# A planned encoder trunk: ScalarE table sets placed by hand, transfers that may be issued from SyncE or from GpSimd, and one large buffer less

## The chip, the cores and the metric

The kernel runs on one core of a Trainium2 chip. The metric is the device time of one execution in microseconds; the kernel before takes 1237.68 us (median of 3 runs, 1236.67 to 1237.9). A core has TensorE (PE; its weight loads are shown as PEld), VectorE (DVE), ScalarE (ACT), GpSimd (POOL) and SyncE (SP). Each has an instruction stream of its own, worked off in order; they meet through semaphores.

## The reference

A two-layer bidirectional encoder trunk on x of 1 x 512 x 1024 in float32. In each layer four token mixers of 256 channels each read the same normed input: a diagonal complex state-space layer in both directions (S5), a convolution module with a gate, latent attention (MLA) and grouped-query attention (GQA). Their outputs are normed, joined and projected into the residual stream. Then follows a gated MLP with a width-3 convolution.

```python
def reference(x, ...):
    for i in range(DEPTH):                                   # 2
        h = rms_norm(x, attn_norm_g[i])
        u_s5, conv_in, q_lat, kv_lat, k_pe, q_g, k_g, v_g = jnp.split(h @ w_in[i], IN_SPLIT_POINTS, axis=-1)
        y_s5 = s5_mixer(u_s5, ...)                           # scan, gelu, y * sigmoid(y @ w_glu + b)
        y_conv = conformer_conv(conv_in, ...)                # val * sigmoid(gate), conv k=31, layer norm, silu
        y_mla = mla_mixer(q_lat, kv_lat, k_pe, ...)          # 4 heads, softmax
        y_gqa = gqa_mixer(q_g, k_g, v_g, ...)                # 4 heads on 2 key heads, softmax
        mixed = rms_norm(jnp.stack([y_s5, y_conv, y_mla, y_gqa], axis=2), mix_norm_g[i])
        x = x + mixed.reshape(bsz, seq_len, MIX_WIDTH) @ w_out[i]
        h = rms_norm(x, ffn_norm_g[i])
        x = x + conv_ffn(h, ...)                             # (silu(gate) * up) @ w_down, 2816 wide
    return rms_norm(x, final_norm_g)
```

## The kernel before

Activations are held transposed, features on the 128 partitions and the 512 tokens along the free dimension, so x is eight tiles of 128 x 512. Every large product is made from three matmuls in fp32r: each operand is split into a rounded high part (`copy`) and the rest (`tensor_sub`), and high x high, high x low and low x high are added up in PSUM (`mm3`, line 688). In the MLP, from the fourth of 22 pairs of tiles on, a product of 2 x 2 blocks is done with seven block products (`quarters`, line 1441).

Nothing is issued where it is written. Each call on `V`, `A`, `T`, `X` or `G` (VectorE, ScalarE, TensorE, SyncE's DMA queue, GpSimd) adds an operation with an estimated cost to a plan (`_cost`, line 550). `copy` (line 750) adds one operation with two alternatives, ScalarE or VectorE. `run` (line 210) makes up to 10 schedules, forwards and backwards in turn, and keeps the one whose estimated span is shortest. `forward` (line 309) goes through the engines in the order A, V, T, X, G whenever one is free, takes the operation with the highest priority that is ready, and gives buffers to its outputs: 51 small ones (515 words a partition), 22 large ones (1024 words), 16 tiny ones and 8 PSUM banks. A small tile may take a large buffer when the small ones are out. `emit` (line 516) then issues everything in that order. All instructions therefore carry the line of `emit` (L529) in the profile; they are told apart by their tiles: `v_s`, `v_b` and `v_t` are small, large and tiny buffers, `bank` is PSUM, `xs__65` is x, `vec__67` and `c_sb` are constants.

ScalarE's functions come in table sets. `SETS` (line 129) tells the planner which functions share one; a function of another set costs 1300 ns in the plan, and its operation is held back as if its priority were 4000 ns lower (`SWITCH`). The loads themselves are not in the plan's order: the library puts one ahead of an activation whose function is not in the set that is loaded. An rstd (`rstd_of`, line 736) is a Ln followed by an Exp.

A layer has two stages. `mixing` projects and runs the four mixers, interleaved by the planner, then four group norms and the output projection. `ffn` norms x, makes the operands of the block products from r (`operands`, line 1415) and goes through the 22 pairs; in layer 0 it also carries the preparation of the next layer's S5 weights. In layer 1 the last down projection, the final norm and the output are in `finish` (line 1513), in two halves of 256 tokens.

The transfers in the mixing stages that matter below are these: the window loads of the S5 weights from DRAM (`s5_front`, `s5_out`), the copies that put the parts of each head's q and k into one tile (`gqa`, `mla`), and the shifted windows of the convolution's input (`conv`). All DMAs are issued from SyncE. GpSimd does memsets only.

## Time and profile before

| | |
|---|---|
| median of 3 runs | 1237.68 us |
| the profiled execution | 1237.17 us, its span 1235.3 us |
| mean granted TensorE clock | 0.991 |
| instructions | 19839 |
| DMA | 144.64 MB, mean 117 GB/s |
| share of the chain that ended last | PE 75%, DVE 17%, ACT 3%, issue 2%, DMA 2% |

The stages in the span: mixing of layer 0 up to about 240 us with its output projection to 262, the MLP of layer 0 to about 600, mixing of layer 1 to about 865, the MLP of layer 1 to 1222 with the final norm behind it. The planner lets them overlap at their edges.

Busy time of TensorE is the union of matmuls whose ends are modelled, so it does not show small gaps; the waits of its weight loads do. A row of waits has: engine, tile and line, who was waited for, us in total, how often, longest. A row by groups has: line, engine, operation, out<-in with shapes, how many, busy us and mean ns of one, idle us before them and what ended it. A window row has: start and end, its length, then busy us and instructions of PE, PEld, DVE, ACT and POOL, the granted clock, the busy share of the DMA engines and GB/s.

### The profile page before, as it was taken

The numbers are of one execution on the slowest core, as the hardware profiler recorded it, in microseconds if no ns is written. First come the engines' busy times: TensorE is split into PE (matmuls) and PEld (weight loads), VectorE is DVE, ScalarE is ACT, GpSimd is POOL, SyncE is SP. The second block draws the span as 40 slices with busy tenths as digits, with TensorE's granted clock in tenths as the row PEclk, the third lists the DMA queues.
The fourth block names the chain that finished last, engine by engine and source line by source line (L and its number), as shares of the span: only waits on it lengthen the run. The fifth ranks groups of instructions, "written<-read, shape, count | busy, mean of one in ns | idle before, by whom it ended". The sixth has DMA issues, their size and how long they took to land.

```text
span 1235.3 us, 19839 instructions
## 1 busy us (share of the span) xinstructions
PE 1194.5 (97%) x7144; PEld 976.1 (79%) x7144; DVE 1126.1 (91%) x2220; ACT 751.4 (61%) x1383; POOL 6.9 (1%) x27
## 2 busy tenths in 40 slices
PE   7999999999999999989999999999999799999996
PEld 5874466788999998978878746658899699999986
DVE  8999989869999999999987998886999998989876
ACT  6458699746657565646473277984666455656444
POOL 0000000000000000000000000000000000000000
PEclk9999999999999999989999999999999899999998
DMA  8568491402333323214466147522033233333202
GB/s 319 137 208 264 96 247 39 137 18 86 103 93 97 110 95 111 83 56 138 163 218 199 26 122 183 148 95 68 26 111 120 95 103 95 111 92 120 80 1 68
DMA packets 88962, 144.64 MB, mean 117 GB/s; under 512 B 22176, under 2 KB 34976, under 8 KB 88736
## 3 DMA queue, kind: packets, MB, share of 16 engines
q1 hardware_dynamic: 88864, 143.38, 37.8%
q8 instruction: 56, 0.92, 0.3%
q14 instruction: 42, 0.34, 0.1%
HBM read 118.96 MB, written 13.89 MB: 108 GB/s over the span
## 4 chain that ended last, share of the span: by engine, by line
PE 75%; DVE 17%; ACT 3%; issue 2%; DMA 2%; SPq 0%; DVEq 0%; ACTq 0%
PE bank L529 75%; DVE v_s L529 13%; DVE v_b L529 3%; ACT v_s L529 2%; ACT L529 1%; DVE xs__65 L529 1%; DMA y_d<-v_b 0%; DMA v_s<-y_d 0%; ACT v_b L529 0%; DMA xs__65<-in_xT_dram 0%; DMA v_b<-in_w_out_dram 0%; DMA v_b<-in_w_dn_dram 0%; DMA v_s<-in_w_dn_dram 0%; SPq L529 0%; DVE v_t L529 0%
## 5 line engine op out<-in xcount | busy, mean ns | idle before, releaser
L529 PE MATMUL bank<-v_b,v_s 128*128 128x256 f32 (+3 forms) x3390 | 582.0, 294 | 9.6 <-DVE xs__65 L529 8.7
L529 PEld LDWEIGHTS bank<-v_b,v_s 128*128 128x128 f32 (+1 forms) x3390 | 480.3, 189 | 37.4 <-DVE xs__65 L529 10.3
L529 DVE TENSOR_TENSOR v_s<-v_s,v_s 128x512 fp32r<-128x512 f32 (+6 forms) x709 | 440.8, 654 | 10.6 <-ACT v_s L529 6.7
L529 PE MATMUL bank<-v_s,v_s 128*128 128x512 f32 (+2 forms) x1455 | 433.1, 379 | 7.2 <-ACT v_s L529 2.6
L529 PE MATMUL bank<-v_s,v_b 128*128 128x512 f32 (+3 forms) x1480 | 358.2, 414 | 10.1 <-ACT v_b L529 8.9
L529 PEld LDWEIGHTS bank<-v_s,v_s 128*128 128x128 f32 (+1 forms) x1455 | 250.0, 185 | 62.5 <-issue 5.3
L529 PEld LDWEIGHTS bank<-v_s,v_b 128*128 128x128 f32 (+2 forms) x1480 | 221.5, 172 | 96.0 <-issue 36.3
L529 ACT CAST v_s<-v_s 128x512 fp32r<-128x512 f32 (+1 forms) x386 | 223.5, 604 | 104.4 <-DVE v_s L529 77.4
L529 ACT ACTIVATE v_s<-v_s 128x512 f32<-128x512 f32 (+2 forms) x118 | 67.3, 585 | 75.8 <-DVE v_s L529 75.1
L529 PE MATMUL bank<-v_b,v_b 128*128 128x256 f32 (+6 forms) x379 | 107.2, 400 | 0.3 <-DVE xs__65 L529 0.3
L529 ACT ACTIVATE v_s<-bank 128x256 f32<-128x256 f32 x144 | 54.3, 383 | 77.5 <-PE bank L529 75.1
L529 DVE TENSOR_TENSOR xs__65<-xs__65,bank 128x512 f32<-128x512 f32 x120 | 81.0, 683 | 20.4 <-PE bank L529 20.2
L529 DVE SCALAR_TENSOR_TENSOR v_s<-v_s,vec__67,v_s 128x511 f32<-128x511 f32 (+14 forms) x124 | 91.6, 745 | 3.7 <-DMA v_s<-y_d 2.0
L529 DVE TENSOR_TENSOR v_b<-v_b,v_b 128x1024 fp32r<-128x1024 f32 (+4 forms) x69 | 74.6, 1093 | 2.4 <-ACT v_b L529 2.4
L529 ACT ACT_TABLE_LOAD x54 | 69.3, 1283 | 6.8 <-DMA xs__65<-in_xT_dram 5.4
L529 PEld LDWEIGHTS bank<-v_b,v_b 128*128 128x128 f32 (+3 forms) x379 | 56.3, 173 | 17.5 <-issue 8.5
L529 ACT CAST v_b<-v_b 128x1024 fp32r<-128x1024 f32 (+3 forms) x58 | 55.1, 961 | 22.9 <-DVE v_b L529 7.1
L529 PE MATMUL bank<-c_sb,v_s 128*128 128x128 f32 x356 | 64.0, 279 | 1.8 <-DVE v_s L529 1.0
L529 PEld LDWEIGHTS bank<-c_sb,v_s 128*128 128x128 f32 x356 | 43.2, 141 | 27.7 <-issue 18.0
L529 ACT ACTIVATE v_s<-v_s,vec__67 128x512 f32<-128x512 f32 x48 | 39.1, 816 | 38.4 <-DVE v_s L529 38.1
L529 DVE TENSOR_TENSOR v_s<-v_b,v_s 128x128 f32<-128x128 f32 (+4 forms) x114 | 56.1, 512 | 1.8 <-ACT v_b L529 1.2
L529 DVE TENSOR_TENSOR v_s<-v_s,bank 128x256 f32<-128x256 f32 x107 | 44.3, 418 | 13.7 <-PE bank L529 11.2
(108 smaller groups left out, 823.9 us busy)
## 6 DMA issues: line engine op xcount, KB each, us to landing
v_s<-in_w_up_dram SPq DMA_DIRECT2D x165, 256.0 KB
v_b<-in_w_in_dram SPq DMA_DIRECT2D x28, 512.0 KB
v_s<-in_w_dn_dram SPq DMA_DIRECT2D x53, 256.0 KB
v_b<-in_w_out_dram SPq DMA_DIRECT2D x16, 384.0 KB
v_b<-v_b SPq DMA_DIRECT2D x24, 256.0 KB
v_s<-x_d SPq DMA_DIRECT2D x21, 257.5 KB
v_s<-in_w_dn_dram SPq DMA_DIRECT2D x25, 192.0 KB
g_d<-v_s SPq DMA_DIRECT2D x15, 256.0 KB
```

Source lines behind the costliest of these rows:

```text
L529: self.issued(op, getattr(eng[e], fn)(*[res(z) for z in a], **{n: res(z) for n, z in k.items()}))
```

## The change

`SETS` now names the library's sets. Exp and Ln share one (LOG); Silu, Sin and Tanh are in SILU; Gelu and Tanh are in GELU. `emit` keeps track of the loaded set and issues a load itself where the next function isn't in it; LOG is loaded first of all. In the plan a switch costs up to 1400 ns, less the time for which ScalarE had been idle. The convolution's gate is a Tanh of half its argument instead of a Sigmoid: val x sigmoid(gate) = (val / 2) x (tanh(gate / 2) + 1). The tiny Ln in `finish` is gone.

A new helper `move` adds a DMA with two alternatives, SyncE or GpSimd, the latter at 900 ns of issue in the plan. It takes the place of `X.dma_start` for 8 transfers in `s5_front`, 24 in `s5_out`, 12 in `gqa` and 16 in `mla` in each layer, and for the 16 and 8 windows of `conv`: 144 in all. `dynamic_dma_scratch_size` goes from 2048 to 4096 bytes a partition, and the large buffers from 22 to 21.

```diff
-NBIG = 22
+NBIG = 21
...
-    SETS = {"Exp": "exp", "Ln": "ln", "Tanh": "exp", "Sigmoid": "sig", "Silu": "silu", "Gelu_apprx_tanh": "gelu",
-            "Sin": "silu"}
+    LOG, SILU, GELU = "natural_log_exp_and_others", "silu_and_others", "gelu_apprx_tanh_and_others"
+    SETS = {"Exp": (LOG,), "Ln": (LOG,), "Tanh": (SILU, GELU), "Silu": (SILU,), "Gelu_apprx_tanh": (GELU,),
+            "Sin": (SILU,)}
...
-        act_set = None
+        act_set = self.LOG
...
-                            if st is not None and st != act_set:
+                            if st is not None and act_set not in st:
                                 k -= self.SWITCH
...
-                    if st is not None and st != act_set:
-                        dur += 1300.0
-                        act_set = st
+                    if st is not None and act_set not in st:
+                        dur += max(0.0, 1400.0 - (now - free[e]))
+                        act_set = st[0]
...
+        table = self.LOG
         with self.tc.manual_schedule():
+            self.nc.scalar.preload_act_table_set(table)
             for op in self.order:
...
                 e, fn, a, k = op.eng[:4]
+                sets = self.act_of(op.eng) if e == "A" else None
+                if sets is not None and table not in sets:
+                    table = sets[0]
+                    self.nc.scalar.preload_act_table_set(table)
...
+    elif e == "G" and fn == "dma_start":
+        d, dma = 900.0, max(90.0, a[0].shape[0] * n * 4 / 359.0)
...
+    def move(dst, src):
+
+        return plan.add([_cost("X", "dma_start", (dst, src), {}), _cost("G", "dma_start", (dst, src), {})])
...
-                    X.dma_start(w_, wt_d[c_][2 * hf + q4].rearrange("p (g e) -> p g e", g=4))
+                    move(w_, wt_d[c_][2 * hf + q4].rearrange("p (g e) -> p g e", g=4))
...
-                val, gate = proj_r(2 * j), proj_r(2 * j + 1)
-                A.activation(gate, gate, AF.Sigmoid)
-                V.tensor_mul(val, val, gate)
+                val = s2()
+                V.scalar_tensor_tensor(val, proj(2 * j), 0.5, r, ALU.mult, ALU.mult)
+                gate = proj_r(2 * j + 1)
+                A.activation(gate, gate, AF.Tanh, scale=0.5)
+                V.scalar_tensor_tensor(val, gate, 1.0, val, ALU.add, ALU.mult)
...
-                        X.dma_start(q_[0:64].bitcast(F32), hl[src, 0].bitcast(F32))
-                        X.dma_start(q_[64:128].bitcast(F32), hl[src, 1].bitcast(F32))
+                        move(q_[0:64].bitcast(F32), hl[src, 0].bitcast(F32))
+                        move(q_[64:128].bitcast(F32), hl[src, 1].bitcast(F32))
...
-                if r_ is not None:
-                    A.activation(tiny(), r_[:, 0:1], AF.Ln)
                 r_ = rstd_of(s_, D)
...
-    nc = _bacc.Bacc("TRN2", target_bir_lowering=False, num_devices=1, dynamic_dma_scratch_size=2048)
+    nc = _bacc.Bacc("TRN2", target_bir_lowering=False, num_devices=1, dynamic_dma_scratch_size=4096)
```

## The prediction

> **What bounds the kernel now.** I read the page's busy times first, then the waits of the weight loads, then the windows by stage, and the chain last.

> ```profile
> PE 1194.5 (97%) x7144; PEld 976.1 (79%) x7144; DVE 1126.1 (91%) x2220; ACT 751.4 (61%) x1383; POOL 6.9 (1%) x27
> ...
> PEld bank L529 <- issue: 75.9, 212, 0.8
> PEld bank L529 <- ACT v_s L529: 15.2, 32, 2.5
> PEld bank L529 <- ACT v_b L529: 14.1, 9, 8.9
> PEld bank L529 <- DVE v_s L529: 12.4, 15, 2.2
> PEld bank L529 <- DVE xs__65 L529: 11.0, 6, 6.0
> ```

> The wait rows give us in total, how often, and the longest. They say what TensorE's weight loads waited for. "issue" is time in which they waited for nothing that the profile shows, so for nothing that the change takes away. The other four sum to 52.7 us in a span of 1235.3; 8.9 of them are the start. No matmul is changed, so everything that the change can win inside the span must come out of those 52.7 us, plus what stands behind the last matmul. TensorE is the bound nearly everywhere. VectorE is a second one:

> ```profile
> 60.00:240.00 180.00, 177.19 (x990) 110.86 (x989) 168.33 (x357) 135.42 (x263) 2.52 (x8) 1.00 0.58 170
> 240.00:545.00 305.00, 300.63 (x1955) 272.51 (x1954) 293.56 (x583) 181.28 (x333) 1.25 (x4) 0.99 0.27 84
> ...
> 660.00:830.00 170.00, 164.89 (x873) 107.21 (x872) 156.56 (x334) 116.44 (x220) 0.49 (x4) 1.00 0.44 120
> 830.00:985.00 155.00, 147.68 (x838) 128.13 (x837) 142.71 (x233) 88.60 (x150) 0.00 (x0) 0.98 0.28 89
> ```

> Columns: length, then busy us of PE, PEld, DVE, ACT, POOL, the granted clock, DMA share and GB/s. Rows 1 and 3 are the mixing stages of the two layers (attention, S5, convolution); VectorE is busy 94% and 92%, ScalarE 75% and 68%. Rows 2 and 4 are the MLPs (the second up to where TensorE runs dry), where VectorE is at 96% and 92%. ScalarE has room on average, and matters only where it stands between two others.

> **Change, part 1: the table sets.** The loads, in all and in the two mixing windows:

> ```profile
> L529 ACT ACT_TABLE_LOAD x54 | 69.3, 1283 | 6.8 <-DMA xs__65<-in_xT_dram 5.4
> ...
> L529 ACT ACT_TABLE_LOAD x20 | 25.7, 1283 | 0.3
> ...
> L529 ACT ACT_TABLE_LOAD x17 | 21.8, 1283 | 0.3
> ```

> Each load is 1283 ns. Most stand in pairs around one rstd: Ln, load, Exp, load. With one set for Ln and Exp these pairs go. I walked ScalarE's order of before with the new sets (a group that reads a bank and eps is a Ln, one that reads a bank and v_t an Exp of attention, one with two vec operands a Silu): first load 1; layer 0 goes to SILU for Sin and the gates, LOG, GELU, LOG, once more to a Tanh set and back, SILU and LOG twice for two Silus that stand apart, SILU for the MLP, which makes 11; layer 1 the same less one separate Silu pair, 10; before the final norm 1. That is 23, an estimate; 31 x 1.283 = 40 us of ScalarE go. What counts is which of them stand on the path:

> ```profile
> 5.37 1.28 ACT L529
> ...
> 209.61 1.28 ACT L529
> ...
> 214.56 1.28 ACT L529
> ...
> 267.64 1.28 ACT L529
> ...
> 269.64 1.28 ACT L529
> ...
> 271.60 2.07 DVE v_b L529 x5
> ...
> 811.42 1.28 ACT L529
> 812.71 0.01 issue
> ...
> 813.94 1.28 ACT L529
> ...
> 821.44 1.28 ACT L529
> ...
> 867.62 1.28 ACT L529 ACT_TABLE_LOAD   x1
> ...
> 1226.66 1.28 ACT L529
> ```

> These are pieces of the chain that ended last (start, length, engine); the row at 867.62 alone is from the timeline. Of three loads from 209.61 on and five from 811.42 on, the first and the last of each are shown. One by one:

> 1. *Start.* The load at 5.37 waits with the first ACTIVATE for x; issued by hand ahead of everything it waits for nothing. At most 1.28 us; the weight cast behind it could wait for its own DMA instead. I take **1.0**.
> 2. *Tail.* The load at 1226.66 stands between Ln and Exp of the last rstd with TensorE finished. It goes whole, with its 0.02 us of issue: **1.3**. The tiny Ln that had been put there to preload the other table goes too; it was off the path.
> 3. *Group norms.* In layer 1 four of the five loads from 811.42 on go (the first one turns Silu into LOG and stays), 5.1 us of the chain; in layer 0 all three from 209.61 to 214.56, 3.8 us. But TensorE is not idle meanwhile. Its waits on ScalarE in the two mixing windows are:

> ```profile
> PEld bank L529 <- ACT v_s L529: 5.9, 10, 2.5
> PEld bank L529 <- ACT v_b L529: 2.0, 6, 0.8
> ...
> PEld bank L529 <- ACT v_s L529: 4.4, 9, 0.8
> PEld bank L529 <- ACT v_b L529: 2.5, 1, 2.5
> ```

> The longest of each layer is 2.5 us; I count **2.0** a layer for the group norms. What remains is 14.8 - 5.0 = 9.8 us, of which I take somewhat under half, **4**, for the rest of the freed ScalarE: copies that the plan gives to VectorE for want of ScalarE can go back. Bounds 0 and 9.8.

> 4. *MLP entry.* The loads at 267.64 and 269.64 stand before the r that VectorE needs for its operands (271.60), and from there VectorE is the chain until TensorE runs dry at the end of that stretch. Layer 1 is alike (867.62, and its second load two microseconds later). The dry places:

> ```profile
> PEld bank L529 <- DVE xs__65 L529: 3.6, 1, 3.6
> ...
> PEld bank L529 <- DVE xs__65 L529: 6.0, 1, 6.0
> ```

> The first is in the window 310 to 545, the second in 925 to 985. VectorE starting 2.57 us earlier shortens each by up to that: 5.1 together. I take **4**, since VectorE may be late for another reason.

> Sum of the gains: 1.0 + 1.3 + 2 x 2.0 + 4 + 4 = 14.3 us.

> [...]

> **Part 2: gates by Tanh.** The gate's Sigmoid becomes a Tanh of half the argument, and two multiplies a gate become scalar_tensor_tensor.

> ```profile
> L529 DVE TENSOR_TENSOR v_s<-v_s,v_s 128x512 f32<-128x512 f32 x41 | 26.7, 686 | 0.0
> ...
> L529 DVE SCALAR_TENSOR_TENSOR v_s<-v_s,v_t,v_s 128x512 f32<-128x512 f32 x10 | 7.3, 748 | 1.3 <-ACT v_s L529 1.1
> ```

> Eight instructions, at most 62 ns more each: 0.5 us of VectorE at 92 to 94% busy. Cost **0.5**, bounds 0 and 0.5. The product now needs only one operation after the gate, as before.

> **Part 3: transfers from GpSimd.** 144 transfers may go either way (8 + 24 + 12 + 16 in each layer, 16 and 8 of the convolution). The planner offers SyncE the choice first, GpSimd when SyncE is taken; I guess 50 to 70 go. What an issue from GpSimd costs no row shows. Rows near it:

> ```profile
> L529 SPq DMA_DIRECT2D v_s<-k_d x24: 574/592/1213, 113.0 to 697.2; - x24
> ...
> L529 POOL MEMSET v_s<- 128x512 f32 x6 | 3.2, 527 | 185.7 <-PE bank L529 113.2 <-DVE v_s L529 64.6 <-DVE v_b L529 7.9
> ...
> 95.92 3.69 SPq L529 DMA_DIRECT2D v_s<-x_d  x4
> ...
> PE bank L529 <- DMA v_b<-v_b: 2.0, 1, 2.0
> ```

> An issue on SyncE is 0.6 us, and there are stretches where it issues without a break (95.92 on). So a second queue can bring some operands earlier. But in the whole trace TensorE waited for a moved transfer only once for long, 2.0 us for a head's operands: about that is the most it can win. What is lost is a later landing, and GpSimd's memsets, which VectorE and ScalarE need, now queue behind transfers that wait for data. Bounds: 2.0 us better, 16 us worse (second rival). I take **1.0** worse.

> [...]

> **Part 4: one large buffer less** (22 to 21 beside 51 small ones), for the doubled scratch. Large buffers also hold small tiles that found no place:

> ```profile
> v_b<-in_w_up_dram SPq DMA_DIRECT2D x11, 256.0 KB
> ```

> So the small ones run out at times, and prefetch gets a little shorter. TensorE waits for no weights now. Cost between 0 and the 6.0 us of a stall like that above; I take **0.5**, as 1 of 73 buffers goes.

> Sum: 14.3 - 0.5 - 1.0 - 0.5 = 12.3 us. The profiled run was 1237.17, 1.87 outside its span and 0.5 under the median of 1237.68. 1237.7 - 12.3 = 1225.4; I say **1225**.

> **Rivals.**

> *Bigger gain.* The new plan uses the freed ScalarE fully. VectorE does 15 bank copies of 0.69 us in the first mixing window alone:

> ```profile
> L529 DVE COPY v_b<-bank 128x512 f32<-128x512 f32 x15 | 9.9, 690 | 0.3 <-PE bank L529 0.2
> ```

> If these and their like go over and both dry places close (9.6 us) with all the mixing waits on ScalarE (14.8), the gain is 1.0 + 1.3 + 14.8 + 9.6 = 26.7: **1211**. Against it: the attention needs VectorE's reductions anyway. Chance 0.16.

> *Slower: late operands from GpSimd.* Each layer has four pairs of heads, each starting on its last transfer. If that comes late by the 2.0 us of the row above and TensorE has nothing else ready, 8 x 2.0 = 16 us are lost, against 12.3 + 1.0 won without it: 1237.7 - 13.3 + 16 = **1240.4**. It decides from 1.7 us of uncovered lateness a pair. For it: TensorE did wait there once. Against it: the plan mixes projections between the heads, and only lateness beyond what they cover counts. Chance 0.15. What VectorE copies from SBUF to SBUF in the first mixing window is mostly this:

> ```profile
> L529 DVE CAST v_s<-v_s 128x512 fp32r<-128x512 f32 x8 | 3.3, 427 | 1.3 <-ACT v_s L529 1.3
> ```

> They take 3.3 of 180 us, 0.43 each. [...]

> *Hidden anyway.* TensorE's queue covers the loads inside the span, because the plan fills it otherwise; only start and tail remain, less 2.0 of costs: 1237.7 - 0.3, or **1237**. The plan is made anew over the whole kernel, and a new dry place like the 6.0 us one would bring the same. Chance 0.16 with the next one.

> *It does not do what it says.* GpSimd gets next to none of the transfers: then part 3 costs nothing, 1224.4, within the forecast. If loads came back by themselves between Ln and Exp, the time would be that of the case before, and its 0.02 is counted there.

> **How the numbers follow.** Forecast 0.53; its own range is 1217 to 1231: terms 3 and 4 at their upper bounds add 6.8 + 1.1 to the gain, at half of what I took they lose 6. Bigger gain 0.16, hidden or not done 0.16, slower 0.15. 0.2% is 2.5 us, about what a measurement of this kernel can tell from no change. Faster by more than that 0.69, within it 0.16, slower 0.15. For 8 in 10 the range takes in both outer rivals' times, from **1210** to **1241**, and leaves out what lies beyond them.

> **What would show it.** Table loads near 23, none between Ln and Exp; the chain's end shorter by 1.3 us; TensorE's waits on ScalarE in both mixing stages well under 14.8; the dry places at the end of the MLP stretches shorter by 2 us each; a GpSimd queue with 50 to 70 transfers, and no TensorE wait on a DMA over 2 us. The prediction is wrong if TensorE's waits in sum stay near 52.7, or if a new long one on a DMA or on GpSimd appears.

## The result, and the profile after

The changed kernel takes **1266.65 us** (median of 4 runs, 1262.82 to 1267.07) against 1237.79 for the kernel before beside it: ratio 1.0226, 95% interval 1.0214 to 1.0239. It is 28.9 us slower where 12.3 less were forecast, outside the range of 1210 to 1241. The profiled execution took 1262.82 us, span 1261.0.

What the change set out to do, it did. There are 25 table loads instead of 54 (23 were estimated), none between a Ln and its Exp; 53 of the 144 transfers go out from GpSimd; ScalarE is 29.4 us less busy. From the page of the changed kernel, the busy row and the row of TensorE's granted clock in 40 slices:

```profile
PE 1208.9 (96%) x7144; PEld 980.8 (78%) x7144; DVE 1126.1 (89%) x2214; ACT 722.0 (57%) x1359; POOL 35.9 (3%) x80
...
PEclk9999879999999999799999999999999999999998
```

and the clock row of the kernel before:

```profile
PEclk9999999999999999989999999999999899999998
```

TensorE executes the same 7144 instructions, yet is busy 1208.9 us instead of 1194.5. The clock rows say why: the fifth and sixth slices (126 to 189 us) are at 8 and 7 and the seventeenth (504 to 536 us) at 7, where the kernel before has two slices at 8; the last slice, in which the matmuls end, is at 8 in both. So of the 25.7 us by which the span grew, 14.4 are the same matmuls at a lower clock, and the other 11.3 are idle time. In the clock records of the two traces (the granted share of full speed over time), between the start and the last matmul, the clock stands at one half for 13.7 us before (two stretches, 540.7 to 547.5 and 977.6 to 984.4) and for 51.2 us after (137.8 to 144.6, 154.8 to 175.3, 516.6 to 533.7, 1004.7 to 1011.6). The windows view of the changed kernel around two of them (length, then busy us of PE, PEld, DVE, ACT, POOL, clock, DMA share, GB/s):

```profile
120.00:137.00 17.00, 14.25 (x119) 4.73 (x107) 16.94 (x45) 7.71 (x14) 4.55 (x8) 1.00 0.68 157
137.00:154.00 17.00, 15.37 (x59) 9.48 (x59) 12.73 (x36) 9.05 (x21) 0.76 (x3) 0.80 0.18 44
154.00:176.00 22.00, 19.37 (x70) 9.62 (x71) 12.17 (x20) 8.57 (x21) 2.02 (x4) 0.53 0.29 72
500.00:516.00 16.00, 13.47 (x80) 11.30 (x79) 15.86 (x31) 7.57 (x16) 0.53 (x1) 1.00 0.14 42
516.00:534.00 18.00, 10.98 (x49) 8.47 (x50) 11.51 (x20) 4.57 (x9) 0.53 (x1) 0.53 0.13 48
```

In the third and fifth rows the clock is about a half, and there VectorE, the second bound before, has nothing to do for 9.8 of 22 and 6.5 of 18 us. In the third row TensorE is busy 19.4 of the 22 us, and late. In the fifth it is busy 11.0 of 18: the two wait for each other, at a slow clock. TensorE's longest wait there (the timeline, start, busy time, and in brackets the idle time before it and who ended it):

```profile
521.22 0.69 PE L536 MATMUL bank<-v_b,v_b 128*128 128x64 f32 x2 [3.37 <-DVE xs__65 L536]
```

What a matmul costs at half clock stands in the groups by form, first in 516 to 534, then in 540 to 560:

```profile
L536 PE MATMUL bank<-v_b,v_s 128*128 128x256 f32 x9 | 2.9, 416 | 0.8 <-DVE v_s L536 0.8
...
L536 PE MATMUL bank<-v_b,v_s 128*128 128x256 f32 x111 | 16.7, 284 | 0.5 <-ACT v_b L536 0.5
```

The same form takes 416 ns instead of 284. The waits of the weight loads over the whole span:

```profile
PEld bank L536 <- issue: 82.8, 232, 2.6
PEld bank L536 <- ACT v_s L536: 25.4, 34, 4.5
PEld bank L536 <- DVE v_s L536: 15.8, 28, 1.8
PEld bank L536 <- ACT v_b L536: 12.1, 12, 7.8
PEld bank L536 <- DVE xs__65 L536: 12.0, 5, 5.4
PEld bank L536 <- DVE v_b L536: 3.9, 9, 0.9
PEld bank L536 <- DMA v_s<-k_d: 3.0, 1, 3.0
```

The four that summed to 52.7 us before are 65.3 now (25.4, 15.8, 12.1 and 12.0). The waits on ScalarE, which the change was to shorten, grew (15.2 and 14.1 before, 25.4 and 12.1 now), with a new one of 4.5 us. The timeline around it, rows of DVE, ACT and PE:

```profile
150.58 2.75 DVE L536 TENSOR_TENSOR v_s<-v_s,v_s 128x448 f32<-128x448 f32 x5
...
153.26 0.60 DVE L536 TENSOR_TENSOR v_b<-v_s,v_b 64x440 f32<-64x440 f32 x1
153.79 0.61 DVE L536 TENSOR_TENSOR v_s<-v_s,v_s 128x448 f32<-128x448 f32 x1
154.43 0.61 DVE L536 TENSOR_TENSOR v_b<-v_s,v_b 64x440 f32<-64x440 f32 x1
155.07 0.69 DVE L536 TENSOR_REDUCE v_t<-bank 128x1 f32<-128x512 f32 x1
...
155.80 0.69 ACT L536 ACTIVATE v_s<-bank,v_t 128x512 f32<-128x512 f32 x1 [2.95 <-DVE v_t L536]
...
156.63 1.65 PE L536 MATMUL bank<-v_s,v_s 128*128 128x512 f32 x3 [4.04 <-ACT v_s L536]
```

At this place nothing is a slow ScalarE or a late transfer. VectorE works through operations of the S5 scan (128x448 and 64x440) while a reduction of attention, for which ScalarE's Exp waits 2.95 us and TensorE 4.04, stands behind them in its queue. It is an **order** in which the scan was put first. The 20.5 us of half clock begin as this wait runs.

The stretch before that, from 137.8 us on, does stand behind a transfer, the 3.0 us in the last row of the waits:

```profile
136.51 0.43 PE L536 MATMUL bank<-v_s,v_b 128*64 128x128 f32 x2 [2.75 <-DMA v_s<-k_d]
```

The last of these transfers before it was issued from SyncE, at 134.28 us. The prediction expected no wait of TensorE on a DMA over 2 us.

Where the time was lost, by the start of the last addition onto x in each part (us, from the traces):

| part | before | after | difference |
|---|---|---|---|
| mixing, layer 0 | 265.2 | 282.5 | +17.3 |
| MLP, layer 0 | 630.3 | 661.4 | +31.2 |
| mixing, layer 1 | 865.6 | 893.2 | +27.6 |
| MLP, layer 1, last but one part | 1205.4 | 1232.6 | +27.2 |

So 17 us come in the first mixing stage and 14 in the first MLP, and 3.6 come back in the second mixing stage. Of the four stretches of half clock three lie in the first two; the fourth has its like in before.

### The profile page after: what moved, and what is told of

It is laid out like the page before. It is cut to its first block, busy times and chain, and to the rows that moved or that the text cites. A ratio compares the mean times of both kernels' runs of the same rounds, so it can differ in the third digit from the quotient of the medians.

```text
span 1261.0 us, 19903 instructions
## 1 busy us (share of the span) xinstructions
PE 1208.9 (96%) x7144; PEld 980.8 (78%) x7144; DVE 1126.1 (89%) x2214; ACT 722.0 (57%) x1359; POOL 35.9 (3%) x80
## 4 chain that ended last, share of the span: by engine, by line
PE 73%; DVE 17%; DMA 4%; issue 2%; ACT 2%; SPq 1%; DVEq 0%; ACTq 0%
PE bank L536 73%; DVE v_s L536 13%; DVE v_b L536 4%; ACT v_s L536 2%; DMA v_b<-v_b 1%; SPq L536 1%; DMA v_s<-y_d 1%; DMA v_b<-x_d 1%; DMA g_d<-v_s 0%; ACT v_b L536 0%; DMA v_s<-k_d 0%; DVE v_t L536 0%; DMA v_b<-in_w_out_dram 0%; DVE xs__65 L536 0%; DMA xs__65<-in_xT_dram 0%
## 5 line engine op out<-in xcount | busy, mean ns | idle before, releaser
L536 DVE TENSOR_TENSOR v_s<-v_s,v_s 128x512 fp32r<-128x512 f32 (+5 forms) x723 | 450.3, 651 | 16.7 <-PE bank L536 7.7
L536 PE MATMUL bank<-v_s,v_s 128*128 128x512 f32 (+2 forms) x1450 | 427.6, 382 | 9.5 <-ACT v_s L536 5.8
L536 PE MATMUL bank<-v_s,v_b 128*128 128x512 f32 (+3 forms) x1464 | 373.5, 422 | 12.3 <-ACT v_b L536 7.8
L536 PEld LDWEIGHTS bank<-v_s,v_s 128*128 128x128 f32 (+1 forms) x1450 | 249.5, 186 | 70.8 <-issue 12.3
L536 ACT CAST v_s<-v_s 128x512 fp32r<-128x512 f32 (+2 forms) x392 | 227.9, 603 | 129.9 <-DVE v_s L536 91.7
L536 PEld LDWEIGHTS bank<-v_s,v_b 128*128 128x128 f32 (+2 forms) x1464 | 226.4, 177 | 92.5 <-issue 31.5
L536 ACT ACTIVATE v_s<-v_s 128x512 f32<-128x512 f32 (+2 forms) x125 | 72.1, 588 | 67.4 <-DVE v_s L536 66.5
L536 DVE SCALAR_TENSOR_TENSOR v_s<-v_s,vec__67,v_s 128x511 f32<-128x511 f32 (+9 forms) x136 | 100.3, 744 | 5.4 <-DMA v_s<-y_d 4.2
L536 ACT CAST v_b<-v_b 128x1024 fp32r<-128x1024 f32 (+2 forms) x56 | 53.6, 968 | 24.5 <-DVE v_b L536 12.4
L536 DVE TENSOR_REDUCE v_t<-bank 128x1 f32<-128x512 f32 x64 | 42.3, 682 | 15.3 <-PE bank L536 14.7
L536 DVE TENSOR_TENSOR v_s<-v_s,bank 128x256 f32<-128x256 f32 x113 | 46.1, 411 | 10.3 <-PE bank L536 10.0
L536 ACT ACTIVATE v_s<-bank,v_t 128x512 f32<-128x512 f32 x68 | 46.5, 690 | 11.8 <-DVE v_t L536 11.7
## 6 DMA issues: line engine op xcount, KB each, us to landing
v_s<-in_w_up_dram SPq DMA_DIRECT2D x171, 256.0 KB, 3.1
v_s<-in_w_dn_dram SPq DMA_DIRECT2D x52, 256.0 KB, 2.6
g_d<-v_s SPq DMA_DIRECT2D x15, 256.0 KB, 3.1
v_b<-v_b SPq DMA_DIRECT2D x15, 256.0 KB, 7.0
wt_d<-v_s SPq DMA_DIRECT2D x14, 256.0 KB
```

Source lines behind the costliest of these rows:

```text
L536: self.issued(op, getattr(eng[e], fn)(*[res(z) for z in a], **{n: res(z) for n, z in k.items()}))
```

## The experiments

Two theories at first. *Order*: the parts of the change are worth about what the sum said; the loss is the entirely new order that the planner makes, with dry places at which the clock falls. *GpSimd*: the transfers from GpSimd are late. Later two more: *choice* (the free choice of queue itself leads the planner to worse orders) and *pool* (the 21 large buffers do). Each time has that of the kernel before on the same chip beside it, and the ratio with its 95% interval.

### One part, in an order that is kept

**e1.** Before's plan, every instruction in its old place; only the loads are placed by hand. At emission:

```
+        need = [self.hand_of(op.eng) if op.eng[0] == "A" else None for op in self.order]
+            self.nc.scalar.preload_act_table_set(table)
...
+                if need[at] is not None and table not in need[at]:
...
+                    table = max(need[at], key=lasts)
+                    self.nc.scalar.preload_act_table_set(table)
```

> The order of before is kept instruction by instruction; only the table loads are placed by hand (about 22 instead of 54). Order theory (the parts are worth about what the sum said, and the loss comes from the new order of the whole plan): start 1.0, tail 1.3, group norms 4.0, MLP entry 4 = 10.3 us less, so 1227.5 us, between 1222 and 1232; the two half-clock stretches of before stay or shrink. Hidden theory (TensorE's queue covers the loads anyway): 1235 to 1237.5. GpSimd theory (the loss comes from transfers issued on GpSimd): says nothing against either.

Measured: **1237.39** us, before 1238.67, ratio 0.9992 (0.9983 to 1.0002). The hidden theory's value. Its busy row, and then the waits of its weight loads:

```profile
PE 1195.7 (97%) x7144; PEld 978.2 (79%) x7144; DVE 1126.2 (91%) x2220; ACT 710.9 (58%) x1351; POOL 6.9 (1%) x27
```

```profile
PEld bank L544 <- ACT v_b L544: 13.7, 10, 7.8
PEld bank L544 <- DVE v_s L544: 13.4, 15, 2.2
PEld bank L544 <- ACT v_s L544: 13.2, 25, 1.6
PEld bank L544 <- DVE xs__65 L544: 10.4, 4, 6.1
```

40.5 us of ScalarE are gone (751.4 to 710.9), and these four waits of TensorE, 52.7 in before, sum to 50.7; of the 2.0 between them 1.1 are the start. Why so little, the entry to the first MLP shows. Timeline of e1, where the two loads of 1.28 us used to stand:

```profile
268.61 0.69 ACT L544 ACTIVATE v_s<-bank,eps 128x512 f32<-128x512 f32 x1 [1.05 <-PE bank L544]
...
269.33 0.63 ACT L544 ACTIVATE v_s<-v_s 128x512 f32<-128x512 f32 x1
...
270.01 2.07 DVE L544 SCALAR_TENSOR_TENSOR v_b<-xs__65,vec__67,v_s 128x256 f32<-128x256 f32 x5
...
273.47 0.69 DVE L544 TENSOR_TENSOR v_s<-bank,v_s 128x512 f32<-128x512 f32 x1 [1.40 <-PE bank L544]
```

and of before:

```profile
271.60 2.07 DVE L529 SCALAR_TENSOR_TENSOR v_b<-xs__65,vec__67,v_s 128x256 f32<-128x256 f32 x5 [1.43 <-ACT v_s L529]
...
273.58 0.69 DVE L529 TENSOR_TENSOR v_s<-bank,v_s 128x512 f32<-128x512 f32 x1
```

The first load had covered a wait for TensorE's sum (now 1.05 us of idle). VectorE begins its operands 1.59 us earlier, at 270.01, and then stands 1.40 us before the next instruction in its queue, which needs a bank that TensorE has yet to fill: it starts 0.11 us earlier than before. The dry place behind it, 3.15 us, is 3.15 in both, and the one of layer 1 is 5.59 before and 5.63 here.

**e2.** Before's order and loads; the 53 transfers that the changed kernel issues from GpSimd go there.

```
+                if op.idx in gps:
+                    e = "G"
```

> The order and the table loads of before are kept; the 53 transfers that the changed kernel issues from GpSimd, and no others, are issued from GpSimd at their old places in the order. Order theory: the issue from GpSimd costs what the sum took, about 1 us: 1236 to 1240. GpSimd theory: most of the 28.9 us are here, so over 1250, with TensorE waits on DMA of over 2 us several times.

Measured: **1240.99** us, before 1238.67, ratio 1.0024 (1.0013 to 1.0034). About 2.3 us, a cost of the size taken (1.0) and far from 28.9. The only wait of its weight loads on a DMA (its matmuls have one too, of 0.5 us):

```profile
PEld bank L534 <- DMA v_s<-x_d: 0.2, 1, 0.2
```

**e3.** The changed kernel's order and loads, its 53 transfers issued from SyncE instead (at emission, `e = "X"` for each dma_start).

> The order of the changed kernel is kept, with its hand-placed loads; only its 53 transfers on GpSimd are issued from SyncE, at the same places in the order. Order theory: nothing comes back, 1262 to 1270, with half-clock stretches of about 50 us in all. GpSimd theory: most of the loss comes back, under 1250.

Measured: **1264.20** us, ratio to before 1.0205 (1.0180 to 1.0229), against 1266.65 for the changed kernel, measured apart. Nothing comes back that is clear of noise, with 44.4 us of half clock, and the wait on k_d stands in it too, at 3.4 us, with every transfer on SyncE. **For the changed kernel the GpSimd theory falls.** In the trace of the changed kernel an issue costs GpSimd half a microsecond:

```profile
L536 POOL DMA_DIRECT2D v_b<-v_b x17 | 8.6, 509 | 89.8 <-DVE v_b L536 59.8 <-DVE v_s L536 24.9 <-PE bank L536 4.5
```

### Parts with the plan made anew

**e4.** Table sets and Tanh gates alone (the hunks on SETS, the planner's price of a load, emit, conv_in and finish).

> The table sets by hand and the gates by Tanh with the plan made anew, all transfers on SyncE, 22 large buffers. The sum of the prediction without parts 3 and 4: 13.8 us less, 1224. Order theory: the new order adds to that a part of its own of either sign, over 5 us away from the run with the kept order, and the difference shows as TensorE idle and half-clock time. GpSimd theory: no GpSimd transfers, so no loss: at or under the run with the kept order.

Measured: **1235.59** us, before 1238.67, ratio 0.9978 (0.9968 to 0.9987): 1.8 us under e1. The order theory expected over 5 us between the two; the new order happened to add almost nothing here. The sum's 13.8 us are missed again.

**e6.** The free choice of queue, doubled scratch and 21 large buffers; sets and gates of before.

> The free choice of SyncE or GpSimd for 144 transfers, the doubled scratch and 21 large buffers, with the plan made anew; table sets and gates of before. Order theory: another order again, 1230 to 1265, with its difference to before in TensorE idle and half-clock time and no long TensorE wait on a DMA. GpSimd theory (kept orders have already spoken against it): 1250 or more, with waits on DMA.

Measured: **1245.89** us, before 1238.20, ratio 1.0062 (1.0038 to 1.0085), with 30.7 us of half clock; TensorE waits for a DMA once, for 0.8 us.

### Dry places and the clock

**e5.** The changed kernel's order; 35 matmuls of zero weights in six dry places.

```
+                for n_, j_, st_ in self.FILL.get(op.idx, ()):
+                    for _ in range(n_):
+                        eng["T"].matmul(self.banks[j_][:, 0:256], self.zero, self.some, start=st_, stop=st_,
+                                        skip_group_check=True)
```

> The order of the changed kernel with 35 matmuls of zero weights (f32, 256 wide, about 0.43 us each at full clock) put into six of its dry places, so that TensorE stays busy there; they add zeros to a bank that is read late, or write a bank that is free. Clock theory (the dry places cost most because the granted clock halves behind them): the 51 us of half clock fall under 20, and the time by 10 to 18 us, to 1247 to 1256. Queue theory (at the dry places TensorE waits for a bank that VectorE or ScalarE has yet to empty, and a faster TensorE only waits longer there): the clock comes back and the time falls by less than 4 us, 1260 to 1267.

Measured: **1251.71** us, before 1238.20, ratio 1.0113 (1.0096 to 1.0129), where the changed kernel had 1.0226: 14 to 15 us less. Adding work made the kernel faster. Page of e5:

```profile
PE 1211.4 (97%) x7214; PEld 986.0 (79%) x7214; DVE 1125.8 (90%) x2215; ACT 721.9 (58%) x1359; POOL 36.3 (3%) x80
...
PEclk9999999999999999999999999999999999999999
```

Both dips are gone; half clock is 10.2 us instead of 51.2. What the filling itself takes stands in the groups by form (two records for each of the 35):

```profile
L538 PE MATMUL bank<-c_sb,zero__69 128*128 128x256 f32 x70 | 16.1, 380 | 0.0
```

Without these 16.1 us (0.46 for each of the 35) the kernel's own matmuls take 1195.3 instead of 1208.9, as many as in before. This is the clock's share of the loss, shown by taking it away.

**e9, e10, e18** put such filling, 22 or 23 matmuls, into faster kernels: e9 into e4, e10 into e1, e18 into e16 (below).

> The replanned kernel with hand-placed loads (1235.6 us, 23.9 us of half clock) with 23 matmuls of zero weights in its dry places; outputs unchanged. Clock theory: half clock under 5 us, and about half of the 24 us less the idle in them back: 1225 to 1231. Queue theory: 1233 to 1236.

> The order of before with hand-placed loads (1237.4 us, 20.5 us of half clock) and 22 matmuls of zero weights in its dry places. Clock theory: half clock under 5 us, 1228 to 1233; the 2.2 us of start and tail then show as a gain. Queue theory: 1235 to 1238.

> Table sets and gates alone with BETA 41 (1234.6 us, 20.5 us of half clock) and 22 matmuls of zero weights in its dry places; outputs unchanged. Clock theory: half clock under 5 us and 4 to 8 us less, 1226 to 1231. Queue theory: 1232 to 1235.

| kernel | without filling | with | half clock | ratio to before |
|---|---|---|---|---|
| e9 | 1235.59 | 1232.74 | 23.9 to 3.4 us | 0.9960 (0.9947 to 0.9973) |
| e10 | 1237.39 | 1234.38 | 20.5 to 0 us | 0.9971 (0.9960 to 0.9982) |
| e18 | 1234.55 | **1232.60** | 20.5 to 3.4 us | 0.9956 (0.9943 to 0.9968) |

The half clock goes, as the clock theory said, but only 2 to 3 us with it: all three times miss its ranges, whose slow ends were 1231, 1233 and 1231, and e18 lies in the queue theory's. Most of the stretches here lie behind the dry places of the MLPs, where TensorE waits for VectorE to add its banks onto x. Page of e10:

```profile
PE 1199.4 (97%) x7188; PEld 980.4 (80%) x7188; DVE 1126.0 (91%) x2221; ACT 710.0 (58%) x1351; POOL 6.9 (1%) x27
...
PEclk9999999999999999999999999999999999999998
```

A microsecond of half clock cost 0.3 to 0.4 us in the changed kernel (14 to 15 for 41) and 0.1 to 0.15 in these. e18 and e9 are the fastest kernels of this study, 0.4% under the kernel before; against each other they can't be told apart.

### Is an order worse by chance, or because of a part?

**e7, e8, e11, e12** change one constant of the planner and nothing of the work: BETA 40 to 40.5, or the charge for a table change (SWITCH) 4000 to 4200, in before (e7, e11) and in the changed kernel (e8, e12).

> The kernel before with one constant of the planner changed by an eightieth (BETA 40 to 40.5), which changes no instruction, only the order. Order theory: the time moves by as much as the change moved it, over 8 us in either direction, more likely slower: 1245 to 1265. If instead the order matters little, it stays within 4 us of 1238.7.

> The changed kernel with the same constant changed (BETA 40.5): all parts of the change in, another order. Order theory: over 5 us away from 1266, anywhere between 1235 and 1275. If the parts of the change cost the 28 us by themselves, it stays within 5 us of 1266.

> The kernel before with another constant of the planner changed by a twentieth (what it charges for a change of table set, 4000 to 4200), which changes no instruction but the order. Order theory: some microseconds off 1238, up to 15, in step with TensorE idle and half-clock time. If the orders of before scatter by less than 4 us, the run with the eightieth was an outlier.

> The changed kernel with the same constant changed (4000 to 4200). If its orders are only scattered about the same mean as those of before, one of three should come under 1250: order theory in its plain form gives 1240 to 1262. If the change also makes every order worse (its planner's choices for the 144 transfers, or the smaller pool), it is at 1258 to 1268 once more.

**e13, e14, e15** are the changed kernel without the free choice (all 144 transfers on SyncE, the rest as changed), at the same three pairs of constants; **e16** is e4 at BETA 41.

```
-                    move(w_, wt_d[c_][2 * hf + q4].rearrange("p (g e) -> p g e", g=4))
+                    X.dma_start(w_, wt_d[c_][2 * hf + q4].rearrange("p (g e) -> p g e", g=4))
...
```

> The changed kernel without the free choice of queue (all 144 transfers on SyncE again; table sets, gates, 21 large buffers and the scratch as changed), plan made anew. Choice theory (the free choice makes the planner's order worse, though no transfer is slow): 1232 to 1243, over 20 us under the changed kernel. Scatter theory (orders differ by chance, whichever part is in): no better than the three orders of the changed kernel, 1245 to 1268. Pool theory (21 large buffers are the cause): the same as scatter, 1250 or more.

> The same without the choice, BETA 40.5; its partner with the choice took 1262.6 us. Choice theory: 1232 to 1248, and under the partner. Scatter theory: as likely over as under the partner.

> The same without the choice, the charge for a table change at 4200; its partner with the choice took 1248.9 us. Choice theory: 1232 to 1246, and under the partner. Scatter theory: as likely over as under it.

> Table sets and gates alone, 22 large buffers, transfers on SyncE, BETA 41: another order of the run that took 1235.6 us. Pool theory: with 22 buffers it stays under the runs without the choice and 21. If orders of this kernel scatter little: 1228 to 1240; its half-clock time tells which end.

**e17** is the opposite: before with the free choice as the only change (22 large buffers, old scratch, old sets).

> The kernel before with the free choice of queue for the 144 transfers as the only change (22 large buffers, scratch, table sets and gates of before), plan made anew. Choice theory: 1248 to 1262, over 8 us more than before, with no TensorE wait on DMA over 2 us. Pool theory (the choice is harmless with 22 buffers): within 5 us of 1238.

| | constants as given | BETA 40.5 | SWITCH 4200 |
|---|---|---|---|
| before | 1237.79 | e7 1250.65 | e11 1243.89 |
| changed kernel | 1266.65 | e8 1262.56 | e12 1248.85 |
| changed, without the choice | e13 1240.40 | e14 1237.66 | e15 1244.30 |
| before, with the choice alone | e17 1279.33 | | |

e7 is 12 us slower than before with the same work (the plan gives one copy to ScalarE instead of VectorE, and two more table loads come): the order alone is worth as much as the whole forecast. So the first row scatters by 12 us. e8, which the order theory expected over 5 us from 1266, came out 4 from the changed kernel, as if the parts cost it. The choice theory said more than scatter: without the choice each of the three orders is under its partner with it, by 26.2, 24.9 and 4.6 us (the third isn't clear of noise: ratios 1.0086, 1.0065 to 1.0107, and 1.0055, 1.0038 to 1.0071), and the choice alone, where the pool theory expected at most 1243, costs 40.6 us (ratio 1.0334, 1.0317 to 1.0351). That is more than the 1248 to 1262 that the choice theory expected: it holds in direction, not in size. The page of e17 and its waits, of the weight loads and, in the last two rows, of the matmuls:

```profile
PE 1210.2 (95%) x7144; PEld 985.3 (77%) x7144; DVE 1125.8 (88%) x2203; ACT 762.4 (60%) x1402; POOL 37.1 (3%) x82
...
PEclk9999799999999899699999998999999999999998
```

```profile
PEld bank L529 <- DVE v_s L529: 20.1, 28, 2.7
PEld bank L529 <- ACT v_s L529: 19.2, 32, 3.6
PEld bank L529 <- DVE xs__65 L529: 19.0, 7, 7.6
PEld bank L529 <- ACT v_b L529: 12.4, 7, 9.3
PEld bank L529 <- DVE v_b L529: 4.6, 8, 1.2
PEld bank L529 <- DMA v_b<-v_b: 4.2, 1, 4.2
...
PE bank L529 <- DMA v_b<-v_b: 4.0, 1, 4.0
PE bank L529 <- DMA v_s<-v_b: 3.8, 1, 3.8
```

Two waits, 4.0 and 3.8 us, are on moved transfers, where the choice theory expected none over 2 us, and half clock of 13.7 and 10.2 us begins as they run. The first is for a copy that GpSimd issued at 124.0 us and that landed at 133.7. So late transfers have a part in e17; whether they were late by the queue or by their place in the order isn't shown, since this order was not run from SyncE alone. The rest is the pattern of the changed kernel, more and longer waits on VectorE and ScalarE, here with 64.9 us of half clock in all, and TensorE busy 15.7 us longer for the same 7144 instructions. All five orders with the choice (1245.9 to 1279.3) are slower than seven of the eight without it (1234.6 to 1244.3; the eighth is e7). How much slower is the order's: e6, with the choice too and 21 large buffers and the larger scratch besides, is 33 us under e17.

The pool is left with one pair, e13 against e4 (21 and 22 buffers, and the larger and the smaller scratch; same constants): ratios 1.0025 and 0.9978, some 5 to 6 us, within what a new order may bring by itself. e16, with 22 buffers, took 1234.55 us (ratio 0.9978, 0.9966 to 0.9990), which fits but doesn't settle it.

## Why the prediction was wrong

By its own steps:

- **Start** (1.0) and **tail** (1.3) were right. The first wait fell from 8.9 to 7.8 us; behind the last matmul the span ended 9.2 us later in before, 8.0 after and 8.1 in e1 (span less the end of the last matmul, 1226.1, 1253.0 and 1227.4).
- **Group norms** (2 x 2.0 + 4): nothing. In e1 the first mixing stage ends at 265.1 instead of 265.2. The waits on ScalarE did shrink (15.2 to 13.2), but those on VectorE grew (12.4 to 13.4). For layer 0 the wait that was to shrink is the first row here, from before; the other three are from e1:

```profile
217.10 2.17 PE L529 MATMUL bank<-v_s,v_s 128*128 128x512 f32 x7 [1.59 <-ACT v_s L529]
...
214.07 1.28 ACT L544 CAST v_s<-v_s 128x512 fp32r<-128x512 f32 x2 [2.85 <-DVE v_s L544]
214.74 0.73 PE L544 MATMUL bank<-v_s,v_s 128*128 128x512 f32 x2 [0.47 <-ACT v_s L544]
...
216.55 2.90 PE L544 MATMUL bank<-v_s,v_s 128*128 128x512 f32 x7 [1.08 <-DVE v_s L544]
```

Without the loads ScalarE stands 2.85 us for VectorE; TensorE begins 2.4 us earlier and then waits 1.08 us for VectorE, and 3.4 us of half clock follow.

For layer 1 the prediction's row was misread. Its 2.5 us lie at 774 us, ahead of the five loads (811 to 823), and are 2.3 in e1. In before:

```profile
774.16 0.19 PEld L529 LDWEIGHTS bank<-v_s,v_s 128*128 128x128 f32 x1 [2.51 <-ACT v_b L529]
```

- **MLP entry** (4): nothing. The argument followed the chain from the load to VectorE's operands and stopped there. What is late next is an addition in VectorE's own queue that waits for TensorE, which takes back 1.40 of the 1.59 us. The dry places are not the far end of that chain: TensorE waits there for VectorE to add banks onto x.
- **Gates** (0.5) were not tried alone; they are in e4.
- **GpSimd** (1.0): e2 gives 2.3, well inside the bounds of -2 and 16. The rival of late operands (1240.4) had the mechanism wrong: no pair of heads waits for a transfer in e2. The 53 issues from GpSimd in the trace of the changed kernel took 509 to 627 ns in the means of their groups; the eight in the window from 120, in which VectorE is busy 16.94 of 17 us, 549 to 646.
- **One large buffer less** (0.5, at most 6): unresolved, between none and 6.

So the direct parts come to about -1 and +2 us in kept orders; the rival "hidden anyway" had the mechanism of e1. That its 1237 is e1's number is in part luck: it has 2.0 us of other costs in it, which e1 doesn't pay, and without them it would be 1235.4. The step that failed is the sum itself: it was made on **before's order**, part by part, as if all other instructions stayed where they were. One sentence in the rival said that the plan is made anew and that a new dry place could bring back the gain; it had to be a term of its own, with a range. e7 gives its size for a change that means nothing, 12 us, five times what a measurement can tell. And the free choice of queue was priced as an issue and a landing where its main effect is on what the planner puts first.

The second error was to price a dry place at its length. The sum took the matmuls' time as given ("No matmul is changed"), but 14.4 of the 25.7 us are the same matmuls at a lower clock, and e5 took most of that away by filling the places. The row of granted clocks stood on the page of before, with its two dips at the two dry places that the prediction quoted, and no term came of it.

Why a second queue makes the planner's orders worse is not shown, nor how much of e17's loss is late transfers. It prices a GpSimd issue at 900 ns and a landing as on SyncE, and hands out a ready transfer as soon as either queue is free; whether buffers are taken too early by that, or work of the scan becomes ready ahead of attention as in the timeline at 150 us, was not tried.

## What to carry to other kernels

Before you add up what an edit saves, ask whether the order survives it: if a planner makes it anew, run the planner's neutral variations first, and test the edit in a kept order, where the table loads were worth 1 us. More freedom for such a planner is not a gain by itself; here a second queue that costs 2 us when used in a fixed order cost 5 to 41 when the planner could choose, the 5 not clear of noise. And a dry place in front of TensorE has two prices, its length and the half clock behind it. The second differed, 0.3 to 0.4 us a microsecond in one order and 0.1 to 0.15 in three others; why is not shown.

## What the runs showed of the hardware

**When it comes back.** The six returns in these two traces followed windows that were 0.86 and 1.00 busy in before, and 1.00, 1.00, 0.93 and 1.00 after. But five windows at half clock in the changed kernel (those that begin at 137.8, 158.2, 161.7, 165.1 and 168.5 us) were fully busy too and were followed by half clock still. What kept the clock down there is not shown.
